# Sixteen experts' weights split by VectorE alone, and a last norm in groups of two and three tiles

## The chip, the core and the metric

The kernel runs on one core of one Trainium2 chip. The metric is the device time of one execution in microseconds (us), lower is better. Three runs of the kernel before took 2844.61, 2835.43 and 2843.97 us, a median of 2843.97.

## The reference

The reference is two transformer blocks over 1024 tokens of width 1024. The change touches only the end of the second one: a mixture of 16 experts in which every expert chooses its 128 tokens, and the norm behind it.

```python
def expert_choice_ffn(h, router_w, w_gate, w_up, w_down):
    cap = EC_CAPACITY * t // N_EXPERTS                    # 2 * 1024 / 16 = 128
    aff = softmax(h @ router_w)
    vals, idx = top_k(swapaxes(aff, 1, 2), cap)           # per expert: its 128 tokens
    xs = h[idx]
    hid = silu(xs @ w_gate) * (xs @ w_up)                 # three 1024 x 1024 matrices
    out = (hid @ w_down) * vals                           # per expert
    return zeros((t, d)).at[idx].add(out)
...
    x = x + g2 * expert_choice_ffn(hx, ...)
    return rmsnorm(x, final_g)
```

All of it is in float32.

## The kernel before, in words

A product in float32 is made of three: TensorE multiplies in a shorter float format (fp32r), so each operand is split into a high half (a copy rounded to that format) and a low half (what is left), and high x high, high x low and low x high are added up in PSUM.

The weights of an expert come in twelve pieces of 1 MB, `[128, 2048]` in float32: four of the gate matrix, four of the up matrix, four of the down matrix. `piece` (lines 254 to 261) loads one through the queue of SyncE into a tile `raw`; ScalarE makes the high half `whi` (line 266); the low half `wlo` is a subtraction (line 269), on VectorE or on GpSimd by the argument `le`. In `product` (line 1784) the pieces 0, 1 and 2 of each matrix have their low half from VectorE and piece 3 has it from GpSimd. Then twelve matmuls of 512 columns use the piece (lines 1792 to 1794). There are eight raw buffers, four for high halves and four for low halves (`k.streams(wp, 8, 4, 4, 2048)`, line 1749). A raw buffer is free for the next load when both halves are made, a half's buffer when TensorE has used it.

Per expert, `route` makes a one-hot matrix on VectorE (`oh`), sixteen narrow matmuls turn it into row numbers and values (`pid`), and GpSimd issues a gather of the 128 rows of `hx` (tile `xg`, 0.5 MB). `to_cm` transposes eight blocks on TensorE and splits them (`xth`, `xtl`). `gate_up` runs the gate product into `pg`, a tanh on ScalarE into `th` (line 1801), a multiply on VectorE (line 1802), the up product into `pu`, and the product of both, `hid`. `to_cm` turns `hid` as well (`hth`, `htl`), and `down` runs the down product of the expert before into `pd`, scales it into `o` on VectorE and lets GpSimd issue a scatter that adds 0.5 MB to the residual in memory. Routing runs three experts ahead.

`last_norm` (line 1837) loads eight tiles of 128 tokens and calls `tm_norm` for each: a sum of squares on ScalarE, a reciprocal root by three Newton steps in `rsqrt` (line 282) on VectorE, a scaling with the gain on VectorE, a store.

The order of the instructions on each engine is fixed when the kernel is built, by a scheduler that simulates the program; what comes later on an engine waits for what stands ahead of it. Which row follows which is thus not in the code, and a small edit can change the order of the whole stage.

Of the kernel before, what the change touches and what calls it, by code (L numbers as in the profile page):

```python
# [7 lines left out]
F32 = mybir.dt.float32  # L8
# [5 lines left out]
OP = mybir.AluOpType  # L14
# [952 lines left out]
def tm_norm(k, pool, xs, gain, shift):  # L967

    nc = k.nc
    n = len(xs)  # L970
    ms = pool.tile([128, n], F32, tag="tms", name="tms")
    junk = pool.tile([128, 1024], F32, tag="njunk", name="tjunk")
# [648 lines left out]
def moe(k, lc):  # L1621
# [126 lines left out]
    wp = lc.enter_context(k.pool("wm"))  # L1748
    k.streams(wp, 8, 4, 4, 2048)
    mb = lc.enter_context(k.pool("mb", side="right"))  # L1750
# [3 lines left out]
    def route(e):  # L1754
# [9 lines left out]
        ts(val, ps[:, 1:2], 0.5, None, op0=OP.mult)  # L1764
        x = mb.tile([128, 1024], F32, tag="xg", bufs=3, name="xg")
        nc.gpsimd.indirect_dma_start(out=x, out_offset=None, in_=d_hx,
# [16 lines left out]

    def product(ps, src, e, h, l, pool=(3,)):
        for p in range(4):
            wh, wl = k.piece(src[e, p], le="pool" if p in pool else "dve")
            for q in range(2):
# [8 lines left out]
    def gate_up(e, h, l):  # L1796
        pg, pu = k.acc("pg"), k.acc("pu")
        hv = lambda z: (z[:, 0:512], z[:, 512:1024])
        product(hv(pg), A["w_g"], e, h, l)
        th = mb.tile([128, 1024], F32, tag="th", name="th")  # L1800
        act(th, pg, AF.Tanh, scale=0.5)
        stt(th, th, 1.0, pg, op0=OP.add, op1=OP.mult)
        product(hv(pu), A["w_u"], e, h, l)
        hid = mb.tile([128, 1024], F32, tag="hid", name="hid")
        for sl in H2:
            tt(hid[:, sl], th[:, sl], pu[:, sl], op=OP.mult)
        return hid

# [10 lines left out]

    R = [route(e) for e in range(3)]  # L1820
    xt = to_cm(R[0][2], "xt")
    prev = None
    for e in range(NE):
# [6 lines left out]
        prev = (e, *to_cm(hid, "ht"), ids, val)  # L1830
        if e + 3 < NE:
            R.append(route(e + 3))
    down(*prev)
# [3 lines left out]
def last_norm(k, d_x3, out):  # L1837
    nc, tc, A = k.nc, k.tc, k.A
    with k.pool("ln") as ln:
        fg = row_bcast(k, ln, A["fg2"], "fg")  # L1840
        for t in range(8):
            z = ln.tile([128, 1024], F32, tag="z", bufs=8, name="z")
            (nc.sync if t % 2 else nc.scalar).dma_start(z, d_x3[128 * t:128 * t + 128, :])
            tm_norm(k, ln, [z], fg, None)
            (nc.scalar if t % 2 else nc.sync).dma_start(out[128 * t:128 * t + 128, :], z)

# [38 lines left out]
```

## Time and profile before

| what | us |
|---|---|
| median of three runs | 2843.97 |
| the profiled execution, its own time | 2840.99 |
| its span in the trace | 2839.1 |
| TensorE busy in the span | 2412.9 (85%) |
| VectorE busy | 1749.7 (62%) |
| ScalarE busy | 1193.3 (42%) |
| GpSimd busy | 1107.7 (39%) |
| low halves on VectorE, 144, busy | 451.1 |

The profile is of one execution, 3 us below the median of the runs. Its shares are means over stages of different kinds, so they say little on the experts; the windows and timelines of the rows below are of that stage and of the last norm alone. In them PE is TensorE, PEld its weight loads, DVE VectorE, ACT ScalarE, POOL GpSimd and SP SyncE. Times are counted from the start of the span. PEclk is the granted clock of TensorE as a share of 2.4 GHz; it has two levels, 1.2 and 2.4 GHz, and a value between is a mean over the window.

### The profile page before, as it was taken

What the parts mean: (1) busy time and instruction counts of PE and PEld (TensorE: products, weight loads), DVE (VectorE), ACT (ScalarE), POOL (GpSimd) and SP (SyncE); (2) the same over time, 40 slices, a digit from 0 to 9 for tenths busy, and PEclk for the clock granted to TensorE, in tenths of its full rate; (3) what the DMA queues carried; (4) which work ended last, traced back from release to release, by engine and by line L of the source; (5) the groups of instructions that cost most, each with busy time, mean ns of one, the idle gap of its engine ahead of it and who ended that gap; (6) DMA issues with size and microseconds to landing.
All of it is one profiled execution on the core that took longest, in us unless ns stands there. A gap on an engine that the chain in (4) does not pass through costs nothing. (4 is left out here: it accounts for less than half of the span.)

```text
span 2839.1 us, 40542 instructions
## 1 busy us (share of the span) xinstructions
PE 2412.9 (85%) x15678; PEld 1982.2 (70%) x15678; DVE 1749.7 (62%) x2631; ACT 1193.3 (42%) x1973; POOL 1107.7 (39%) x863
## 2 busy tenths in 40 slices
PE   5789997888689976989997778889958999999982
PEld 4556786677568965877776666667847887777772
DVE  7064727766323375122657768564776998899885
ACT  3133432222222152324636665632324666556562
POOL 5111214432344255342636454342313545444442
PEclk8879997888889987999985665669968999999996
DMA  4355321111254332435212122257455999998884
GB/s 179 53 185 171 105 82 46 36 62 53 86 179 137 134 117 95 157 134 156 77 58 77 40 75 66 65 168 235 171 237 195 369 368 340 319 324 320 328 324 141
DMA packets 220284, 458.53 MB, mean 162 GB/s; under 512 B 45631, under 2 KB 139903, under 8 KB 195516
## 3 DMA queue, kind: packets, MB, share of 16 engines
q1 hardware_dynamic: 203868, 406.80, 41.7%
q0 software_dynamic: 6240, 21.10, 2.8%
q10 hardware_dynamic: 9984, 28.05, 2.5%
q8 instruction: 123, 2.02, 0.3%
q14 instruction: 69, 0.57, 0.1%
HBM read 370.03 MB, written 77.22 MB: 158 GB/s over the span
## 5 line engine op out<-in xcount | busy, mean ns | idle before, releaser
L269 POOL TENSOR_TENSOR wlo<-raw,whi 128x1024 fp32r<-128x1024 f32 (+1 forms) x135 | 451.7, 3348 | 762.0 <-ACT whi L266 741.1
L266 ACT ACTIVATE whi<-raw 128x2048 fp32r<-128x2048 f32 (+1 forms) x279 | 456.0, 1648 | 446.0 <-PE prest L278 94.8
L269 DVE TENSOR_TENSOR wlo<-raw,whi 128x2048 fp32r<-128x2048 f32 x144 | 451.1, 3163 | 54.2 <-ACT whi L266 54.2
L277 PE MATMUL prest<-hTh,whi 128*128 128x512 f32 x448 | 181.8, 406 | 4.4 <-ACT ev L376 4.4
L278 PE MATMUL prest<-hTl,whi 128*128 128x512 f32 x448 | 178.4, 398 | 0.0
L279 PE MATMUL prest<-hTh,wlo 128*128 128x512 f32 x448 | 178.1, 398 | 0.0
L1793 PE MATMUL pg<-wlo,xth 128*128 128x512 f32 x256 | 109.7, 428 | 28.9 <-POOL wlo L269 25.7
L1794 PE MATMUL pg<-whi,xtl 128*128 128x512 f32 x256 | 107.6, 420 | 2.5 <-DVE xtl L1781 2.5
L1792 PE MATMUL pg<-whi,xth 128*128 128x512 f32 x256 | 108.4, 423 | 0.0
L863 DVE SCALAR_TENSOR_TENSOR ac<-raw,sc,ac 128x1024 f32<-128x1024 f32 x64 | 91.4, 1442 | 26.2 <-DMA raw<-in_ada_w 23.5
L1793 PE MATMUL pd<-wlo,hth 128*128 128x512 f32 x256 | 102.1, 399 | 5.0 <-DVE wlo L269 4.6
L277 PEld LDWEIGHTS prest<-hTh,whi 128*128 128x128 f32 x448 | 86.9, 194 | 23.7 <-ACT ev L376 5.3
L1793 PE MATMUL pu<-wlo,xth 128*128 128x512 f32 x256 | 101.1, 395 | 0.0
L1794 PE MATMUL pu<-whi,xtl 128*128 128x512 f32 x256 | 100.6, 393 | 0.0
L1794 PE MATMUL pd<-whi,htl 128*128 128x512 f32 x256 | 100.5, 393 | 0.0
L1792 PE MATMUL pu<-whi,xth 128*128 128x512 f32 x256 | 100.4, 392 | 0.0
L279 PEld LDWEIGHTS prest<-hTh,wlo 128*128 128x128 f32 x448 | 86.4, 193 | 18.8
L278 PEld LDWEIGHTS prest<-hTl,whi 128*128 128x128 f32 x448 | 86.4, 193 | 17.4
L1792 PE MATMUL pd<-whi,hth 128*128 128x512 f32 x256 | 92.5, 394 | 2.5 <-ACT whi L266 2.5
L469 DVE CUSTOM_DVE_ANT_0 sc<-psc,bt 128x384 f32<-128x384 f32 (+1 forms) x64 | 32.7, 520 | 99.4 <-DMA bt<-d_f 52.4
L277 PE MATMUL px<-h2h,whi 128*128 128x512 f32 x224 | 90.6, 404 | 1.2 <-ACT px L1022 1.2
L1031 DVE SCALAR_TENSOR_TENSOR mix<-px,omu,mix 128x1024 f32<-128x1024 f32 (+1 forms) x23 | 23.2, 1013 | 110.8 <-ACT mix L1030 107.4
(583 smaller groups left out, 6883.9 us busy)
## 6 DMA issues: line engine op xcount, KB each, us to landing
raw<-in_w_g SPq DMA_DIRECT2D x64, 1024.0 KB, 6.0
raw<-in_w_u SPq DMA_DIRECT2D x64, 1024.0 KB, 6.9
raw<-in_w_d SPq DMA_DIRECT2D x64, 1024.0 KB, 6.2
raw<-in_w_in SPq DMA_DIRECT2D x69, 512.0 KB, 3.4
raw<-in_ada_w SPq DMA_DIRECT2D x48, 512.0 KB, 3.3
x<-in_x SPq DMA_DIRECT2D x16, 512.0 KB, 5.8
d_g<-ev SPq DMA_DIRECT2D x32, 256.0 KB, 3.1
gt<-d_g SPq DMA_DIRECT2D x16, 512.0 KB, 5.0
```

The lines of the kernel that those rows point to most:

```text
L266: nc.scalar.activation(hi, src, AF.Copy)
L269: (nc.gpsimd if le == "pool" else nc.vector).tensor_tensor(lo, src, hi.bitcast(F32), op=OP.subtract)
L277: mm(ps, wh[:, c], xh[:, kt, sl], start=kt == 0, stop=False)
L278: mm(ps, wh[:, c], xl[:, kt, sl], start=False, stop=False)
L279: mm(ps, wl[:, c], xh[:, kt, sl], start=False, stop=kt == kts - 1)
L469: nc.vector.tensor_tensor_reduce(sc[:, :W], pss[g][:, :W], bt[:, 4 * g + i, c0:c1], 1.0, -3e38, op0=OP.add, op1=OP.max, accum_out=MX[g][:, ...
L863: nc.vector.scalar_tensor_tensor(ac, raw, sc[:, 8 * w + p:8 * w + p + 1], ac, op0=OP.mult, op1=OP.add)
L1031: nc.vector.scalar_tensor_tensor(xv, body[:, :, 0:W], k.omu[:, mu:mu + 1], xv, op0=OP.mult, op1=OP.add)
L1792: mm(o, h[:, kt], wh[:, c], start=kt == 0, stop=False)
L1793: mm(o, h[:, kt], wl[:, c], start=False, stop=False)
L1794: mm(o, l[:, kt], wh[:, c], start=False, stop=kt == 7)
```

## The change

Five edits, four of them in the expert stage:

- All low halves of the experts' weights are made by VectorE; `product` loses its argument.
- The ring of raw tiles has eleven buffers instead of eight; the rings of high and of low halves have three instead of four.
- Two gathered tiles `xg` instead of three, and routing runs two experts ahead instead of three.
- `hid` has no tile of its own: the product of `th` and `pu` is written over `th`.
- `last_norm` loads its eight tiles first, and calls `tm_norm` for groups of 2, 3 and 3 tiles; `tm_norm` then makes the reciprocal roots of a group in one chain on tiles of two and three columns. The tile of mean squares gets two buffers per group size.

```diff
@@ tm_norm
-    ms = pool.tile([128, n], F32, tag="tms", name="tms")
+    ms = pool.tile([128, n], F32, tag=f"tms{n}", bufs=2, name="tms")
@@ moe
-    k.streams(wp, 8, 4, 4, 2048)
+    k.streams(wp, 11, 3, 3, 2048)
...
-        x = mb.tile([128, 1024], F32, tag="xg", bufs=3, name="xg")
+        x = mb.tile([128, 1024], F32, tag="xg", bufs=2, name="xg")
...
-    def product(ps, src, e, h, l, pool=(3,)):
+    def product(ps, src, e, h, l):
         for p in range(4):
-            wh, wl = k.piece(src[e, p], le="pool" if p in pool else "dve")
+            wh, wl = k.piece(src[e, p], le="dve")
...
         product(hv(pu), A["w_u"], e, h, l)
-        hid = mb.tile([128, 1024], F32, tag="hid", name="hid")
         for sl in H2:
-            tt(hid[:, sl], th[:, sl], pu[:, sl], op=OP.mult)
-        return hid
+            tt(th[:, sl], th[:, sl], pu[:, sl], op=OP.mult)
+        return th
...
-    R = [route(e) for e in range(3)]
+    R = [route(e) for e in range(2)]
...
-        if e + 3 < NE:
-            R.append(route(e + 3))
+        if e + 2 < NE:
+            R.append(route(e + 2))
@@ last_norm
+        xs = []
         for t in range(8):
             z = ln.tile([128, 1024], F32, tag="z", bufs=8, name="z")
             (nc.sync if t % 2 else nc.scalar).dma_start(z, d_x3[128 * t:128 * t + 128, :])
-            tm_norm(k, ln, [z], fg, None)
-            (nc.scalar if t % 2 else nc.sync).dma_start(out[128 * t:128 * t + 128, :], z)
+            xs.append(z)
+
+        t = 0
+        for n in (2, 3, 3):
+            tm_norm(k, ln, xs[t:t + n], fg, None)
+            for i in range(t, t + n):
+                (nc.scalar if i % 2 else nc.sync).dma_start(out[128 * i:128 * i + 128, :], xs[i])
+            t += n
```

The order of the instructions up to the expert stage is the same in both kernels. In it, the scheduler orders every engine anew. On VectorE, in the middle of the stage, from the multiply behind one expert's tanh, before:

```order
L1802 SCALAR_TENSOR_TENSOR th<-th,pg 128x1024
L269 TENSOR_TENSOR wlo<-raw,whi 128x2048
L1806 TENSOR_TENSOR hid<-th,pu 128x512 x2
L269 TENSOR_TENSOR wlo<-raw,whi 128x2048 x2
L1781 TENSOR_TENSOR htl<-ptc,hth 128x512 x2
L269 TENSOR_TENSOR wlo<-raw,whi 128x2048
L1763 CAST ids<-pid 128x1
L1764 TENSOR_SCALAR val<-pid 128x1
L1756 TENSOR_TENSOR oh<-rcst,slotT 128x1024
L269 TENSOR_TENSOR wlo<-raw,whi 128x2048
```

and in the changed kernel, from the same multiply of an expert in the middle (the second `th` is the product written over it, `o` is made of the two PSUM tiles `pd`):

```order
L1802 SCALAR_TENSOR_TENSOR th<-th,pg 128x1024
L269 TENSOR_TENSOR wlo<-raw,whi 128x2048 x4
L1805 TENSOR_TENSOR th<-th,pu 128x512 x2
L269 TENSOR_TENSOR wlo<-raw,whi 128x2048 x3
L1814 SCALAR_TENSOR_TENSOR o<-pd_20423,val,g_17672 128x512
L269 TENSOR_TENSOR wlo<-raw,whi 128x2048
L1814 SCALAR_TENSOR_TENSOR o<-pd_20424,val,g_17672 128x512
L269 TENSOR_TENSOR wlo<-raw,whi 128x2048
L1781 TENSOR_TENSOR xtl<-ptc,xth 128x512 x2
L1781 TENSOR_TENSOR htl<-ptc,hth 128x512
L269 TENSOR_TENSOR wlo<-raw,whi 128x2048
L1781 TENSOR_TENSOR htl<-ptc,hth 128x512
```

Twelve low halves an expert stand there instead of nine, four of them instead of one between the multiply and the product with `pu`; and pairs like `xtl` and `htl` come next to each other.

On TensorE, where the stage begins, one set of row-number matmuls less stands ahead of the first transposes:

```order
 L1743 MATMUL psl<-cst,nm 128x128
-L1760 MATMUL pid<-ta,oh 128x2 x24
+L1760 MATMUL pid<-ta,oh 128x2 x16
 L1778 MATMUL ptc<-cst,xg 128x128 x8
 L1792 MATMUL pg<-whi,xth 128x512
```

The third set and each later one comes in the gate product of the expert before the one it is for. In two of the early experts 61 matmuls of 512 columns stand between it and the transposes of the rows gathered by it; in the others more, in the kernel before a whole expert more.

On VectorE, where the last norm begins, behind the last scaling of a down product, before:

```order
L1815 SCALAR_TENSOR_TENSOR o<-pd_23006,val,g_17672 128x512
L975 TENSOR_SCALAR tms<-tms 128x1
L288 TENSOR_SCALAR rsi<-tms 128x1
L289 TENSOR_SCALAR rsy<-rsi 128x1
L292 TENSOR_SCALAR rst<-rsy,tms 128x1
L296 TENSOR_SCALAR rst<-rst 128x1
L297 TENSOR_TENSOR rsy<-rsy,rst 128x1
```

and in the changed kernel, where one chain serves two tiles:

```order
L1814 SCALAR_TENSOR_TENSOR o<-pd_22987,val,g_17672 128x512
L975 TENSOR_SCALAR tms<-tms 128x2
L288 TENSOR_SCALAR rsi<-tms 128x2
L289 TENSOR_SCALAR rsy<-rsi 128x2
L294 TENSOR_TENSOR rst<-rsy 128x2
L295 TENSOR_TENSOR rst<-rst,tms 128x2
L296 TENSOR_SCALAR rst<-rst 128x2
L297 TENSOR_TENSOR rsy<-rsy,rst 128x2
```

A chain has twelve small instructions before and fifteen after; there were eight chains and there are three.

## Rows read from the trace of the kernel before

**Rows 1.** The timeline of ScalarE: start us, us, engine, line, operation, out<-in, count, [idle before <-releaser]
```profile
2187.46 1.03 ACT L1801 ACTIVATE th<-pg 128x1024 f32<-128x1024 f32 x1 [0.80 <-PE pg L1794]
...
2375.24 1.03 ACT L1801 ACTIVATE th<-pg 128x1024 f32<-128x1024 f32 x1 [0.33 <-PE pg L1794]
...
2755.49 1.02 ACT L1801 ACTIVATE th<-pg 128x1024 f32<-128x1024 f32 x1 [6.01 <-PE pg L1794]
```

**Rows 2.** Windows of one expert: window, us; per engine busy us (instructions); PEclk, DMA share, GB/s
```profile
2263.20:2300.40 37.20, 36.74 (x179) 30.36 (x178) 34.30 (x22) 25.82 (x18) 19.20 (x6) 1.00 0.98 370
2506.40:2549.20 42.80, 39.37 (x177) 31.95 (x177) 38.92 (x22) 25.53 (x17) 18.98 (x5) 0.93 0.92 324
```

**Rows 3.** The timeline of all engines where the expert stage begins
```profile
2136.87 10.37 PE L1760 MATMUL pid<-ta,oh 128*128 128x2 f32 x48 [1.72 <-DVE oh L1756]
...
2152.62 0.39 PE L1792 MATMUL pg<-whi,xth 128*128 128x512 f32 x1
...
2152.82 1.92 ACT L266 ACTIVATE whi<-raw 128x2048 fp32r<-128x2048 f32 x1 [3.13 <-PE pg L1794]
...
2154.77 2.29 DVE L269 TENSOR_TENSOR wlo<-raw,whi 128x2048 fp32r<-128x2048 f32 x1 [4.36 <-ACT whi L266]
...
2160.55 0.39 PE L1794 MATMUL pg<-whi,xtl 128*128 128x512 f32 x1
```

**Rows 4.** The timeline of TensorE, early expert: transposes, row-number matmuls
```profile
2283.79 1.03 PE L1778 MATMUL ptc<-cst,hid 128*128 128x128 f32 x8
...
2292.86 1.84 PE L1760 MATMUL pid<-ta,oh 128*128 128x2 f32 x16
```

**Rows 5.** The timeline of all engines in a late expert
```profile
2538.55 7.69 DVE L269 TENSOR_TENSOR wlo<-raw,whi 128x2048 fp32r<-128x2048 f32 x1
...
2538.95 5.13 POOL L269 TENSOR_TENSOR wlo<-raw,whi 128x2048 fp32r<-128x2048 f32 x1
...
2544.13 0.79 PE L1793 MATMUL pg<-wlo,xth 128*128 128x512 f32 x1 [2.82 <-POOL wlo L269]
```

**Rows 6.** The tile raw, VectorE: duration ns min/median/max, first and last start us
```profile
L269 DVE TENSOR_TENSOR wlo<-raw,whi x144: 2273/2281/7710, 2086.2 to 2780.9; 128x2048 fp32r<-128x2048 f32 x144
```

**Rows 7.** Groups by line and form, VectorE: count | busy us, mean ns | idle before
```profile
L269 DVE TENSOR_TENSOR wlo<-raw,whi 128x2048 fp32r<-128x2048 f32 x144 | 451.1, 3163 | 54.2 <-ACT whi L266 54.2
...
L295 DVE TENSOR_TENSOR rst<-rst,tms 128x4 f32<-128x4 f32 x6 | 1.0, 162 | 0.2
```

**Rows 8.** The waits of ScalarE, 2080 to 2800 us: us in total, times, longest
```profile
ACT whi L266 <- DMA raw<-in_w_g: 3.8, 2, 2.1
```

**Rows 9.** The timeline of VectorE in an early expert
```profile
2314.39 1.28 DVE L1781 TENSOR_TENSOR xtl<-ptc,xth 128x512 fp32r<-128x512 f32 x2
...
2327.00 1.40 DVE L1815 SCALAR_TENSOR_TENSOR o<-pd,val,g 128x512 f32<-128x512 f32 x2
...
2335.40 0.15 DVE L1763 CAST ids<-pid 128x1 uint32<-128x1 f32 x1
...
2336.67 2.28 DVE L269 TENSOR_TENSOR wlo<-raw,whi 128x2048 fp32r<-128x2048 f32 x1
2338.87 1.21 DVE L1802 SCALAR_TENSOR_TENSOR th<-th,pg 128x1024 f32<-128x1024 f32 x1
```

**Rows 10.** DMA issues, 2320 to 2360 us: count, median us to landing
```profile
xg<-d_hx,ids POOLq DMA_INDIRECT x1, 12.7
```

**Rows 11.** The timeline of ScalarE, then of VectorE, in the last norm
```profile
2803.54 1.06 ACT L974 ACTIVATE tjunk<-z 128x1024 f32<-128x1024 f32 x1 [23.20 <-DMA z<-d_x]
...
2807.42 1.28 DVE L978 SCALAR_TENSOR_TENSOR z<-z,rsy,fg 128x1024 f32<-128x1024 f32 x1
2808.62 0.15 DVE L975 TENSOR_SCALAR tms<-tms 128x1 f32<-128x1 f32 x1
...
2834.26 1.28 DVE L978 SCALAR_TENSOR_TENSOR z<-z,rsy,fg 128x1024 f32<-128x1024 f32 x1
```

**Rows 12.** Windows, as in the second group: the first pieces are loaded
```profile
2090.00:2094.00 4.00, 2.48 (x11) 2.21 (x12) 3.85 (x5) 1.34 (x3) 0.00 (x0) 0.50 1.02 430
```

## The prediction

> **What bounds the kernel now.** I read the 40 slices of the page first: from the 31st on TensorE and VectorE are 8 to 9 tenths busy and the DMA moves over 300 GB/s. That is the expert stage, and all that the change touches lies there and in the last norm behind it.
>
> Then the stage by itself. Each expert has one tanh on ScalarE after its gate product; from the second (2187.46) to the sixteenth (2755.49) are 568.0 us, 14 intervals, a mean of 40.57 us [rows 1]. They are of two kinds. The first five, up to 2375.24, take 37.6 on average, the last nine 42.3. The windows of one expert each show the difference [rows 2]: from 2263.2 on 37.2 us, TensorE busy for 36.7 and its granted clock 1.00 (2.4 GHz); from 2506.4 on 42.8, TensorE idle for 3.4 and its clock 0.93.
>
> What is TensorE's floor? An expert has 144 matmuls of 512 columns. Between 2152.62 and 2160.55 stand 35 of them at full clock: 0.2266 us each [rows 3], so 32.6 us. Two sets of eight transposes at 1.03 and sixteen row-number matmuls at 1.84 [rows 4] make 36.5 us. The early pattern is 0.6 us above that floor, the late window 6.3.
>
> Why the later one? In the waits TensorE stands longest before a low half of a weight that GpSimd writes: 2.82 us at 2544.13 [rows 5]. With one such stall an expert the 6.3 us are explained: 2.8 of stall, and a mean clock of 0.93 says that 0.07 / 0.5 = 14% of the window, 6.0 us, ran at the lower level of 1.2 GHz, which loses 3.0 more. The cause is seen in the same rows: a low half on VectorE, begun at 2538.55, takes 7.69 us while GpSimd's own runs 5.13 us beside it; without such company the median is 2.281 us [rows 6]. The 144 low halves of VectorE take 451.1 us [rows 7]; at 2.281 they would take 328.5. So 122.6 us of VectorE's time is nothing but waiting for GpSimd's reads.
>
> Weights in transit do not bound it: ScalarE waited 3.8 us in all for a raw piece [rows 8].
>
> **The change part by part.**
>
> *Low halves.* 48 of 192 go from GpSimd to VectorE (three of twelve an expert). VectorE's new work per expert: from the start of a lone low half to the next instruction is 2.20 us (2336.67 to 2338.87), twelve are 26.4; row numbers, values and one-hot 1.27 (2335.40 to 2336.67); three pairs like xtl, at 1.28 less the 0.08 by which neighbours overlap, 3.6; the pair o 1.32; the multiply after the tanh 1.13 [rows 9]. Sum 33.7 us, below TensorE's 36.5. Before, it was 38.9 us in a late expert [rows 2]. So VectorE takes on 48 instructions and still gets lighter, since GpSimd no longer reads anything in this stage; TensorE stays the bound.
>
> The Trainium skill speaks against this: its page Perfetto Trace Analysis, section Optimizing Scalar/DVE Operations, says that a saturated VectorE may do well to hand work to ScalarE or even GpSimd. That page of the Trainium skill adds that the two share a read port, so that it might not help. Rows 5 and 6 side with the addition; had the first half held, the time would be that of the fifth rival below.
>
> *Rings of three instead of four for high and low halves.* This is the price. A high half may be written when TensorE is through with the piece whose buffer it takes. Rows 3 show that loop uncontended: TensorE ends the first piece at 2152.8, ScalarE starts at 2152.82 (1.92 us), VectorE at 2154.77 (2.29 us), ready at 2157.06; TensorE wants it four pieces after the first began, right behind the last matmul at 2160.55, so about 2161.0. Margin 3.9 us. With three buffers it is one piece (2.72 us) less: 1.2 us. VectorE's other jobs push into this: a pair of 1.2 to 1.4 us between two low halves, less the 0.5 us that VectorE has free per piece, costs 0.9 of the 1.2. Two pairs in a row, which the new order has once or twice an expert, cost 1.4 to 2.1: a stall of 0.2 to 0.9 us. The tanh delays the next high half by 1.03 us, but the multiply on VectorE then runs beside that high half. So I expect up to 0.6 us of stalls an expert; the first window of rows 2 has 0.46 us of idle TensorE in it and kept a clock of 1.00. Bounds: 0 to 5 us an expert. I take the pace of the early pattern, 37.1 us, which has the floor plus 0.6: 14 x (40.57 - 37.1) = 48.6 us saved.
>
> *Raw ring of eleven.* ScalarE hardly waited for raw pieces, so three more hide little: 0 to 3.8 us [rows 8]; I take 0. The DMA must move 12.6 MB of weights and 1.05 MB of gather and scatter in 37.1 us, 368 GB/s, which the early pattern did [rows 2].
>
> *Two gathered tiles instead of three.* Routing one expert less ahead removes eight of the 24 pairs of row-number matmuls before the first product, at most a third of 10.37 us [rows 3]. The first gather has to land too, so I take 1.5 us of the 0 to 3.4. The other side: a gather is now used within the same expert. In two early experts 61 matmuls, 13.8 us, stand between its row numbers and its transposes, and it lands 12.7 us after its issue [rows 10], with up to 1 us before that. Bounds 0 to 6 us of stall; I take 2.
>
> *hid into th.* The product overwrites th, so the next tanh waits for the transposes of it; in the new order those stand half a product or more ahead of it on TensorE. Nothing; if they came late, ScalarE would be held behind them and the loop above with it.
>
> *Last norm.* VectorE's chain alone sets this end. Eight tiles are 3.83 us apart (2807.42 to 2834.26 in seven steps): 1.20 us of scaling, to 2808.62, and 2.64 us for twelve small instructions, 0.22 each [rows 11]. After: three rounds of 15 at 0.22 (a form of four columns takes 0.162 us [rows 7], no more than one column), 9.9, and eight scalings, 9.6: 19.5 instead of 30.7, 11.2 less. The first round waits for a second sum of squares, 1.06 us on ScalarE [rows 11] and its read-out. I take 10.0 us. The last three stores are now 1.2 us apart instead of 3.8, which may give back some tenths.
>
> Sum: 48.6 - 2 + 1.5 + 10.0 = 58.1 us. The profiled execution took 2840.99 us, span 2839.1; 2841.0 - 58.1 = 2782.9. The median of the runs shown is 2843.97, 3 us above it and within their spread of 9 us.
>
> **The rivals.**
>
> 1. *The rings of three stall.* If every expert has two or three stalls of 1 us, as two-pair places with a late high half would give, the pace is 38.5 to 41.5 us: 2802 to 2844 us, say 2817 at 39.6. For it: a margin of 1.2 us against pairs of 1.3. Against it: in the new order each wait of VectorE on TensorE is for the same piece whose end also frees the next high half, so the two run side by side.
> 2. *The clock goes with it; slower than before.* Place: two pairs in a row on VectorE before a low half. Price: when such a stall grows to the 2.82 us of 2544.13 [rows 5], the lower clock after it costs 3.0 more, as worked out from rows 2. At 1.3 such places an expert the pace is 36.5 + 1.3 x 5.8 = 44.0 and the time 2841 + 14 x 3.4 - 9.5 = 2879. It decides from a pace of 41.3 on, where the stage gives back what start and end gain. Against it: GpSimd's 5 us splits made that stall, and they are gone.
> 3. *Transfers become the bound.* At the floor, 13.65 MB in 36.5 us are 374 GB/s. With the DMA share at 0.98 in the early window [rows 2] it may be at its end at 370, a pace of 36.9: nothing lost. The Trainium skill's page SBUF — State Buffer, section Summary: rules for kernel authors, puts HBM to SBUF transfers at about 358 GB/s; by it, an estimate, the pace would be 38.1 and the time 2797; the trace does not agree. Against it: 430 GB/s while the first pieces were loaded [rows 12].
> 4. *Only the end moves.* If the later pattern's stalls have another cause than GpSimd, the stage stays and 2830 remains. The 2.82 us row names GpSimd, so this is unlikely.
> 5. *VectorE keeps its mean of 3.16 us a low half* [rows 7]. Then an expert has 12 x 3.13 + 7.3 = 45 us of VectorE and the time is about 2890. Against it: a median of 2.281 in the same row as the 7.71.
>
> **How the numbers follow.** Forecast, pace 36.5 to 38.5, 2766 to 2802: 0.62. Rival 1: 0.20, a tenth of it within 0.3% of before. Rival 2: 0.06. Rival 3: 0.05. Rival 4: 0.05. Rival 5: 0.02. About 0.3%, 8.5 us, is what a measurement of this kernel can tell. Faster: 0.62 + 0.18 + 0.05 + 0.05 = 0.90; same 0.02; slower 0.08. Low end: the floor of 36.5 in all 14 intervals (57 us), 3.4 at the start, 11.2 at the end give 2769, less 3 for the spread of the runs. High end: 2818, the middle of rival 1. Between lies nearly 0.8.
>
> **What would show it.** Right: tanh to tanh near 37 us up to the last expert; a clock of 0.98 or more in those windows; 192 low halves on VectorE with a mean under 2.35 us; GpSimd with gathers and scatters alone; 11 to 12 us less from the first to the last scaling in the last norm. Wrong: waits of TensorE for low halves summing to over 30 us, with high halves behind them waiting on TensorE; transposes waiting for a gather in more than two experts; ScalarE waiting for raw pieces.

## The result, and the profile after

The changed kernel takes 2799.84 us (median of four runs, 2797.09 to 2807.33). Four runs of the kernel before, beside it, have a median of 2841.09. The ratio is 0.9864, with a 95% interval of 0.9844 to 0.9884: faster by 1.4%, some 41 us. The forecast was 2782.9 with a range of 2766 to 2818. So the sign and the range hold, but 17 us of the expected 58 did not come.

The two profiled executions, 2840.99 and 2797.09 us, are compared stretch by stretch. The marks are the matmul psl, which ends the routing tables, the tanhs of [rows 1], the last output product's o, and the span's end:

| stretch | before, us | after, us | difference, us | forecast, us |
|---|---|---|---|---|
| start to psl (same program) | 2134.7 | 2139.0 | +4.3 | 0 |
| psl to the second tanh | 52.8 | 49.7 | -3.1 | -1.5 |
| second to sixteenth tanh, 14 intervals | 568.0 | 535.5 | -32.5 | -46.6 |
| sixteenth tanh to the last o | 35.7 | 34.2 | -1.5 | 0 |
| last o to the end | 47.9 | 36.9 | -11.0 | -10.0 |

The shortfall lies in the 14 intervals: 14.1 us. Here are the tanhs that end them on both sides, in the timeline of ScalarE of the changed kernel, to be held against [rows 1]:

```profile
2188.68 1.03 ACT L1801 ACTIVATE th<-pg 128x1024 f32<-128x1024 f32 x1 [1.03 <-PE pg L1794]
...
2724.17 1.03 ACT L1801 ACTIVATE th<-pg 128x1024 f32<-128x1024 f32 x1 [1.02 <-PE pg L1794]
```

The intervals, in order: 38.14, 36.37, 36.38, 36.42, 37.30, **42.54**, 36.37, **42.46**, 36.35, **42.32**, 36.55, 37.30, **42.29**, 34.70. They are not spread around the forecast of 37.1. Eight are 36.35 to 37.30, better than the forecast or within 0.2 us of it, and four cost 42.3 to 42.5. The windows of one expert of each kind, after (columns as in [rows 2]):

```profile
2299.60:2336.00 36.40, 36.40 (x177) 30.38 (x176) 34.75 (x25) 25.75 (x18) 5.16 (x2) 1.00 1.00 384
2373.29:2415.83 42.54, 38.34 (x177) 31.61 (x176) 33.80 (x25) 26.01 (x17) 5.16 (x2) 0.96 0.94 343
```

In the first TensorE is busy for all of 36.40 us. In the second it idles for 4.2, and its granted clock is 0.96. What it waited for, between 2130 and 2770 us (us in total, times, longest):

```profile
PE ptc L1778 <- DVE xtl L1781: 12.1, 6, 2.6
PE pg L1792 <- ACT xth L1780: 6.4, 4, 1.6
...
PE pd L1793 <- DVE wlo L269: 0.3, 1, 0.3
```

TensorE's waits for low halves are gone (0.3 us), and VectorE's low halves have lost their company; the tile's group on VectorE after, against [rows 6, 7] (duration in ns: least, median, most):

```profile
L269 DVE TENSOR_TENSOR wlo<-raw,whi x192: 2278/2287/2296, 2090.6 to 2754.1; 128x2048 fp32r<-128x2048 f32 x192
```

In their place stands a new wait, at the transposes of gathered rows and the split (xth, xtl) of what they give. This is TensorE's timeline in the expert of 42.54 us:

```profile
2394.63 0.40 PE L1794 MATMUL pd<-whi,htl 128*128 128x512 f32 x1
2394.86 1.04 PE L1778 MATMUL ptc<-cst,xg 128*128 128x128 f32 x8
2397.51 0.50 PE L1792 MATMUL pg<-whi,xth 128*128 128x512 f32 x1 [1.61 <-ACT xth L1780]
2397.85 0.40 PE L1793 MATMUL pg<-wlo,xth 128*128 128x512 f32 x1
2400.84 0.92 PE L1778 MATMUL ptc<-cst,th 128*128 128x128 f32 x4 [2.59 <-DVE xtl L1781]
...
2402.41 0.63 PE L1793 MATMUL pg<-wlo,xth 128*128 128x512 f32 x1
```

The eight transposes of xg stand behind the last matmul of the output product and directly in front of the gate product that needs them. TensorE has nothing else in its order, so it sits through the whole chain: 1.61 us for xth, then 2.59 for xtl. ScalarE comes to xth late, because in its order a high half of a weight stands ahead of it; this high half itself began when TensorE was through with an earlier piece:

```profile
2395.06 1.91 ACT L266 ACTIVATE whi<-raw 128x2048 fp32r<-128x2048 f32 x1 [0.81 <-PE pd L1794]
2396.88 1.07 ACT L1780 ACTIVATE xth<-ptc 128x512 fp32r<-128x512 f32 x2
```

VectorE comes to xtl late as well, because in its order two low halves and an o come first:

```profile
2395.04 2.28 DVE L269 TENSOR_TENSOR wlo<-raw,whi 128x2048 fp32r<-128x2048 f32 x1
2397.24 0.74 DVE L1814 SCALAR_TENSOR_TENSOR o<-pd,val,g 128x512 f32<-128x512 f32 x1
2397.90 2.28 DVE L269 TENSOR_TENSOR wlo<-raw,whi 128x2048 fp32r<-128x2048 f32 x1
2400.10 1.28 DVE L1781 TENSOR_TENSOR xtl<-ptc,xth 128x512 fp32r<-128x512 f32 x2
```

Windows around that place (columns as before) show what the clock added:

```profile
2398.20:2400.80 2.60, 0.04 (x1) 0.00 (x0) 2.60 (x3) 0.00 (x0) 2.54 (x1) 1.00 1.03 366
2400.80:2404.50 3.70, 3.66 (x11) 3.04 (x12) 1.27 (x2) 0.60 (x1) 0.84 (x1) 0.54 0.99 343
2404.50:2407.20 2.70, 2.70 (x13) 2.21 (x12) 0.00 (x0) 1.78 (x1) 0.00 (x0) 1.00 1.01 296
```

After 2.6 us in which TensorE was busy for 0.04, it is granted 0.54 for 3.70 us, near the lower level of 1.2 GHz: 3.70 x 0.46 = 1.7 us lost. With the 4.2 of waiting that is 5.9 us, the difference between 42.4 and 36.4. The windows of all four such experts have a clock of 0.96: together 24 us.

They are not waiting for the gather: this tile's gather was issued at 2370.85 and landed 9.5 us later, about 14 us before its transposes ran. Behind the first expert the least time between a landing and its transposes was 1.3 us.

Start and end did a little more than forecast. At the start TensorE has 32 row-number matmuls instead of 48, but the transposes behind them then wait 2.25 us (put down to oh, which was done 0.8 us earlier; the gather, issued at 2145.84, landed 4.3 us later, just before they began):

```profile
2141.17 6.96 PE L1760 MATMUL pid<-ta,oh 128*128 128x2 f32 x32 [1.72 <-DVE oh L1756]
2150.37 1.94 PE L1778 MATMUL ptc<-cst,xg 128*128 128x128 f32 x8 [2.25 <-DVE oh L1756]
```

So the first product gained nothing: its tanh came 26.3 us behind psl before and 26.8 after. The gain lies between the first tanh and the second, 26.44 us before and 22.87 after. The first tanh, before and after:

```profile
2161.03 1.03 ACT L1801 ACTIVATE th<-pg 128x1024 f32<-128x1024 f32 x1 [0.85 <-PE pg L1794]
2165.81 1.03 ACT L1801 ACTIVATE th<-pg 128x1024 f32<-128x1024 f32 x1 [0.80 <-ACT xth L1780]
```

At the end, VectorE's last o and the three groups of scalings, against [rows 11]:

```profile
2758.37 1.43 DVE L1814 SCALAR_TENSOR_TENSOR o<-pd,val,g 128x512 f32<-128x512 f32 x2 [1.98 <-PE pd L1794]
...
2776.04 2.48 DVE L978 SCALAR_TENSOR_TENSOR z<-z,rsy,fg 128x1024 f32<-128x1024 f32 x2
...
2781.88 3.68 DVE L978 SCALAR_TENSOR_TENSOR z<-z,rsy,fg 128x1024 f32<-128x1024 f32 x3
...
2787.84 3.68 DVE L978 SCALAR_TENSOR_TENSOR z<-z,rsy,fg 128x1024 f32<-128x1024 f32 x3
```

### The profile page after: what moved, and what is told of

Its sections match the earlier page's. It is cut to its first block, busy times and chain, and to the rows that moved or that the text cites. A ratio compares the mean times of both kernels' runs of the same rounds, so it can differ in the third digit from the quotient of the medians.

```text
span 2795.3 us, 40451 instructions
## 1 busy us (share of the span) xinstructions
PE 2400.2 (86%) x15678; PEld 1979.2 (71%) x15678; DVE 1712.1 (61%) x2628; ACT 1197.3 (43%) x1973; POOL 873.1 (31%) x815
## 4 chain that ended last, share of the span: by engine, by line
PE 55%; DVE 19%; ACT 6%; DMA 5%; issue 5%; POOL 3%; SPq 0%; ACTq 0%; DVEq 0%; POOLq 0%
PE pg L1794 2%; PE pg L1792 2%; PE pg L1793 2%; PE px L277 2%; PE px L278 2%; PE px L279 2%; PE pu L1793 2%; PE pu L1792 2%; PE pu L1794 2%; PE prest L277 2%; PE prest L278 2%; PE prest L279 1%; DVE wlo L269 1%; PE pd L1794 1%; PE pd L1793 1%
## 5 line engine op out<-in xcount | busy, mean ns | idle before, releaser
L269 DVE TENSOR_TENSOR wlo<-raw,whi 128x2048 fp32r<-128x2048 f32 x192 | 435.8, 2288 | 59.3 <-ACT whi L266 58.8
L269 POOL TENSOR_TENSOR wlo<-raw,whi 128x1024 fp32r<-128x1024 f32 x87 | 216.6, 2492 | 491.7 <-ACT whi L266 468.5
L1815 POOL DMA_INDIRECT d_x<-o,ids x16 | 51.6, 3227 | 417.7 <-DVE o L1814 417.7
L1793 PE MATMUL pg<-wlo,xth 128*128 128x512 f32 x256 | 102.8, 402 | 0.0
L469 DVE CUSTOM_DVE_ANT_0 sc<-psc,bt 128x384 f32<-128x384 f32 (+1 forms) x64 | 32.6, 519 | 95.4 <-DMA bt<-d_f 52.6
```

Source lines behind the costliest of these rows:

```text
L269: (nc.gpsimd if le == "pool" else nc.vector).tensor_tensor(lo, src, hi.bitcast(F32), op=OP.subtract)
L469: nc.vector.tensor_tensor_reduce(sc[:, :W], pss[g][:, :W], bt[:, 4 * g + i, c0:c1], 1.0, -3e38, op0=OP.add, op1=OP.max, accum_out=MX[g][:, ...
L1793: mm(o, h[:, kt], wl[:, c], start=False, stop=False)
L1815: nc.gpsimd.indirect_dma_start(out=d_x3, out_offset=bass.IndirectOffsetOnAxis(ap=ids[:, :1], axis=0), in_=o, in_offset=None, compute_op=OP ...
```

## The experiments

The theory: GpSimd's low halves were the cost that the change removes, and the four late experts come from where the transposes of gathered rows stand. With route(e+2) called at the end of expert e's turn, the scheduler, so the theory goes, takes the gather to be late and puts the transposes behind the output product; what the scheduler reckons with is on no record. Rivals: the rings of three halves, the raw ring, the weights' transfers, the count of gathered tiles.

Eleven kernels ran. The stretch up to psl, the same program in all but the last two rows, began its last matmul anywhere from 2127.9 to 2146.7 us, so the stretches behind it tell more than the whole time. The time is the median of all runs of a kernel, and the ratio is to runs of the kernel before beside them (medians 2840.18 to 2846.53); psl and the stretches are of the one profiled execution. All in us:

| kernel | time, median | ratio to before, 95% | psl | psl to 2nd tanh | 14 intervals | 16th tanh to end |
|---|---|---|---|---|---|---|
| before | | | 2134.7 | 52.8 | 568.0 | 83.6 |
| after | 2799.84 | 0.9864 (0.9844 to 0.9884) | 2139.0 | 49.7 | 535.5 | 71.1 |
| e1_dve | 2792.93 | 0.9826 (0.9807 to 0.9845) | 2142.0 | 51.2 | 515.2 | 83.2 |
| e3_norm | 2836.98 | 0.9986 (0.9969 to 1.0003) | 2139.7 | 54.7 | 563.9 | 73.4 |
| e4_xg3 | 2769.80 | 0.9754 (0.9729 to 0.9778) | 2127.9 | 50.2 | 513.9 | 70.9 |
| e6_xg3_844 | 2784.07 | 0.9788 (0.9768 to 0.9808) | 2131.4 | 52.6 | 515.0 | 72.5 |
| e7_raw8 | 2792.35 | 0.9805 (0.9774 to 0.9836) | 2139.0 | 50.5 | 529.5 | 72.2 |
| e5_ring844 | 2797.77 | 0.9828 (0.9798 to 0.9857) | 2144.4 | 51.8 | 531.2 | 72.4 |
| e10_early | 2781.35 | 0.9780 (0.9753 to 0.9806) | 2146.7 | 55.0 | 513.1 | 70.8 |
| e2_pool3 | 2865.52 | 1.0074 (1.0049 to 1.0099) | 2138.9 | 53.0 | 590.8 | 81.6 |
| e11_r833 | 2854.12 | 1.0031 (1.0014 to 1.0048) | 2136.8 | 53.9 | 571.1 | 90.9 |
| e8_rw | 2885.15 | 1.0127 (1.0092 to 1.0162) | 2174.7 | 69.4 | 576.5 | 71.0 |
| e9_wo | 2790.00 | 0.9800 (0.9768 to 0.9832) | 2152.8 | 50.1 | 516.0 | 70.9 |

**e1_dve: the low halves alone.**

```diff
-            wh, wl = k.piece(src[e, p], le="pool" if p in pool else "dve")
+            wh, wl = k.piece(src[e, p], le="dve")
```

> The kernel before with one edit: VectorE makes every low half; the ring of eight raw tiles, the rings of four halves, the three gathered tiles and the old last norm stay. Theory (the low half is worth the pace, and what the change lost, about 6 us in each of four experts, comes from gathering only two experts ahead): the low halves take 2.29 us each, no wait of TensorE on them is left, and all 14 intervals between tanhs come out at 36.3 to 37.3 us, none at 42; the stage loses 14 x 4.1 = 57 us and about 3 at its start, so the time is 2841 - 60 = 2781 us (2774 to 2790). Rival A (the raw ring of eight is too short for a VectorE that no longer waits, so TensorE waits for weights): intervals of 38 to 40, 2800 to 2825 us. Rival B (the four late experts come from the memory, not from the gathers): intervals of 42 appear here too, in 3 to 5 experts, and the time is 2800 to 2812 us.

One edit takes 52.8 us from the 14 intervals, more than the whole change did (32.5). No interval is longer than 38.3, though three are above the 37.3 that I expected. One expert's window:

```profile
2267.94:2304.37 36.43, 36.43 (x177) 30.34 (x176) 34.17 (x25) 25.77 (x17) 5.16 (x2) 1.00 1.00 378
```

Both rivals fall. The time itself is 12 us above what was expected and outside its range; 7 of these lie before psl in the profiled execution, where nothing was changed.

**e3_norm: the last norm alone** (the buffers of the means in tm_norm, and last_norm, on the kernel before).

```diff
-            tm_norm(k, ln, [z], fg, None)
...
+        for n in (2, 3, 3):
+            tm_norm(k, ln, xs[t:t + n], fg, None)
```

> The kernel before with the last norm of the change alone (tiles in groups of two, three and three, two buffers for the means). Theory: the time from the last output product's o to the span's end falls from 47.9 to 37 us, and nothing before it moves: 2841 - 11 = 2830 us (2826 to 2834), a ratio of 0.996. Rival (the end is set by the last scatters and the reload of d_x3, so the norm itself is hidden): 0.999 to 1.000, and the stretch after the last o stays above 45 us.

The last o stands at 2794.00, and the span ends at 2831.7: 37.7 us, 10.2 less than before. The scalings, in VectorE's timeline, follow as in the changed kernel:

```profile
2794.00 1.43 DVE L1815 SCALAR_TENSOR_TENSOR o<-pd,val,g 128x512 f32<-128x512 f32 x2 [8.05 <-PE pd L1794]
2812.22 2.48 DVE L978 SCALAR_TENSOR_TENSOR z<-z,rsy,fg 128x1024 f32<-128x1024 f32 x2
...
2824.27 3.68 DVE L978 SCALAR_TENSOR_TENSOR z<-z,rsy,fg 128x1024 f32<-128x1024 f32 x3 [0.29 <-DVE rsy L297]
```

In the trace the term is as expected. The whole time is inconclusive: its median lies 3 us above its range, and its interval takes in 1.000 and just misses the expected 0.996. e1_dve and e6_xg3_844, which run the stage alike (515.2 and 515.0 us) and differ in this norm, are 8.9 us apart.

**e4_xg3 and e6_xg3_844: three gathered tiles again**, with rings of (10, 3, 3), and of (8, 4, 4).

```diff
-        x = mb.tile([128, 1024], F32, tag="xg", bufs=2, name="xg")
+        x = mb.tile([128, 1024], F32, tag="xg", bufs=3, name="xg")
...
-    R = [route(e) for e in range(2)]
+    R = [route(e) for e in range(3)]
...
-        if e + 2 < NE:
-            R.append(route(e + 2))
+        if e + 3 < NE:
+            R.append(route(e + 3))
```

> The changed kernel with three gathered tiles and routes three experts ahead as before the change, a raw ring of ten (11 doesn't fit beside the third tile) and rings of three halves. Theory (an expert takes 42 us where the transposes of the gathered rows stand directly in front of the gate product that uses them, and they stand there because the gather is placed only two experts ahead): the transposes stand inside the output product in all experts, no interval of 42 us is left, all are 36.3 to 37.3, and the time is 2797 - 4 x 6 = 2773 us (2768 to 2781). Rival A (the rings of three halves make the late experts): three to five intervals of 42 stay, 2793 to 2803 us. Rival B (the weights' transfers make them): the same times as rival A, with TensorE's waits ended by a DMA.

> The changed kernel with three gathered tiles, routes three ahead and the rings of before (eight raw, four and four halves): so the change without its rings and without its two gathered tiles. Theory (the gathers decide, the rings do nothing): the same as the run with ten raw tiles, within 4 us: 2773 us (2768 to 2781), intervals of 36.3 to 37.3. Rival A (the rings of three halves make the late experts): this one is faster than the run with rings of three by 15 us or more. Rival B (the longer raw ring is worth something once VectorE makes all low halves): this one is slower than the run with ten raw tiles by 8 us or more, with waits of TensorE ended by DMA.

Both stages came out alike, 513.9 and 515.0 us in the 14 intervals, with none over 39.2: the rings of three cost nothing here, and the longer raw ring gives nothing. (They differ in both rings at once, so one could hide what the other does.) The transposes no longer wait for xtl; the largest wait of TensorE left in e4_xg3 is small:

```profile
PE pg L1793 <- DVE wlo L269: 4.9, 5, 1.4
```

e4_xg3 came out within its range. e6_xg3_844 is 3 us above its own and its median 14 us above that of e4_xg3, which rival B would have at 8 or more; but no wait of TensorE in the stage is ended by a DMA, as rival B wants, and the two ratios' intervals overlap. Of the 8.6 us between the two profiled executions 3.5 lie before psl, 4.0 in the start and the end and 1.1 in the 14 intervals; the rest of the 14 is not explained. e4_xg3, at 0.9754, beats both kernels, and its interval does not touch that of the changed kernel.

**e7_raw8: two gathered tiles, transposes elsewhere.** The raw ring goes from eleven to eight, and with it the scheduler's order: the transposes now stand 10 to 36 matmuls before the end of the output product.

```diff
-    k.streams(wp, 11, 3, 3, 2048)
+    k.streams(wp, 8, 3, 3, 2048)
```

> The changed kernel with a raw ring of eight in place of eleven, and nothing else: two gathered tiles and rings of three halves as in the change. In its order on TensorE the transposes of gathered rows stand inside the output product in all experts but the first, with at least 10 matmuls of that product behind them, and never directly in front of the gate product. Theory (the place of these transposes makes the four late experts, not the count of gathered tiles by itself): no interval of 42 us is left, the 14 intervals sum to 512 to 520 us (changed kernel 535.5; three gathered tiles 513.9), and the time is 2797 - 18 = 2779 us (2768 to 2788). Rival A (the gather itself is late with two tiles, wherever the transposes stand): TensorE waits for the gathered tile or behind it, and the sum stays at 530 us or more. Rival B (eleven raw tiles are needed once VectorE makes all low halves): intervals of 38 to 40 with waits ended by DMA, a sum of 535 or more.

No interval of 42 is left, but the sum is 529.5: my 512 to 520 was too low, and so was the range of the time. Four intervals are 39.48, each where 12 matmuls of the product follow the transposes. TensorE, then VectorE, in one of them:

```profile
2470.38 1.03 PE L1778 MATMUL ptc<-cst,xg 128*128 128x128 f32 x8
...
2476.51 0.50 PE L1793 MATMUL pg<-wlo,xth 128*128 128x512 f32 x1 [1.68 <-DVE wlo L269]
```
```profile
2471.64 0.69 DVE L1781 TENSOR_TENSOR xtl<-ptc,xth 128x512 fp32r<-128x512 f32 x1 [2.04 <-ACT xth L1780]
...
2474.17 2.28 DVE L269 TENSOR_TENSOR wlo<-raw,whi 128x2048 fp32r<-128x2048 f32 x1
```

VectorE comes to xtl in its order and idles 2.04 us for the late transposes, with a low half queued behind; TensorE then waits 1.68 us for that low half. So late transposes hurt along a second path. The distance on TensorE alone does not decide: one expert with 10 matmuls behind them took 36.23 us. The rivals as put do not hold either, though the sum is close to that of rival A: in the intervals one wait of TensorE, of 0.7 us, is ended by the gather, and none by a weight's transfer.

**e5_ring844: two gathered tiles, long rings of halves** (the changed kernel with the rings of before).

```diff
-    k.streams(wp, 11, 3, 3, 2048)
+    k.streams(wp, 8, 4, 4, 2048)
```

> The changed kernel with the rings of before (eight raw, four and four halves); two gathered tiles as in the change. In its order on TensorE the transposes of gathered rows stand directly in front of the gate product in five experts, with one matmul between in a sixth and four in a seventh (changed kernel: four). Theory (that place costs about 6 us each time): five to seven intervals of 41 to 43 us, a sum of 14 intervals of 509 + 5.5 x 6 = 542 us (538 to 552), and a time of 2797 + 7 = 2804 us (2798 to 2818), although its rings of halves are longer. Rival A (the rings of three halves make the late experts): the sum falls to 512 to 518 us, as in the runs with three gathered tiles.

531.2 us, between theory and rival. Three intervals of 40.3 to 40.4 and two of 38.6 to 38.8 show the late place; none is 42. One of them, in the timelines of TensorE, ScalarE and VectorE, and its expert's window:

```profile
2520.77 0.50 PE L1792 MATMUL pg<-whi,xth 128*128 128x512 f32 x1 [0.25 <-ACT xth L1780]
...
2523.29 0.76 PE L1778 MATMUL ptc<-cst,th 128*128 128x128 f32 x4 [1.78 <-DVE xtl L1781]
```
```profile
2520.12 1.09 ACT L1780 ACTIVATE xth<-ptc 128x512 fp32r<-128x512 f32 x2 [1.24 <-PE ptc L1778]
```
```profile
2520.35 2.28 DVE L269 TENSOR_TENSOR wlo<-raw,whi 128x2048 fp32r<-128x2048 f32 x1
2522.55 1.28 DVE L1781 TENSOR_TENSOR xtl<-ptc,xth 128x512 fp32r<-128x512 f32 x2
```
```profile
2497.92:2538.32 40.40, 38.37 (x177) 31.59 (x176) 34.44 (x25) 26.01 (x17) 5.16 (x2) 0.96 0.97 342
```

The waits are 0.25 and 1.78 us, where the changed kernel has 1.61 and 2.59. The same place on TensorE costs 6 us in the changed kernel and 2 to 4 here. So short rings do not make the late experts. Their price goes by what stands ahead of the splits: here ScalarE waits for the transposes and takes xth at once, and VectorE has one low half behind their start ahead of xtl; in the changed kernel a high half stands ahead of xth, and two low halves and an o ahead of xtl. Rings and orders changed together, and no run tells which of the two sets the price.

**e10_early: two gathered tiles, the route called earlier.**

```diff
     for e in range(NE):
+        if e + 2 < NE:
+            R.append(route(e + 2))
         ids, val, x = R[e]
...
-        if e + 2 < NE:
-            R.append(route(e + 2))
```

> The changed kernel (eleven raw tiles, rings of three, two gathered tiles) with one edit: route(e+2) is called at the head of expert e's turn, before its gate product, not at the end of the turn. The tile that it fills was last read by the transposes for expert e, so it is free by then. On TensorE the transposes of gathered rows then stand inside a product everywhere, with at least ten matmuls behind them. Theory (the place of the gather and of the transposes makes the late experts, neither the count of gathered tiles nor the rings of halves): no interval of 42 us is left, 14 intervals sum to 513 to 518 us (changed kernel 535.5, three gathered tiles 513.9), and the time is 2797 - 20 = 2777 us (2766 to 2784). Rival A (two gathered tiles are too few, wherever the route stands): TensorE's transposes wait for the gathered tile, or intervals of 39 to 42 stay, and the sum is 525 us or more. Rival B (with rings of three and late transposes, as in the run with eight raw tiles, VectorE falls behind): intervals of 39.5 with waits of TensorE for low halves, a sum of 525 to 532 us.

513.1 us, the lowest of all, with the changed kernel's rings and two tiles. An expert's window:

```profile
2313.46:2349.84 36.38, 36.38 (x177) 30.39 (x176) 34.38 (x25) 25.78 (x18) 5.94 (x2) 1.00 0.98 368
```

So neither the rings nor the count of tiles by itself makes the late experts; where the route is called does. The call moves two things, the gather's time and the order; since the gathers had landed in time in the changed kernel too, the order is what is left. The start gives some back (55.0 us to the second tanh, as expert 2's row numbers now stand ahead of the end of the first gate product). The median of 2781.35 us is above that of e4_xg3, but the two ratios' intervals overlap.

**e2_pool3 and e11_r833: GpSimd's low halves with the short rings.** The first gives the last piece of each product back to GpSimd in the changed kernel; the second gives the kernel before rings of (8, 3, 3).

```diff
-            wh, wl = k.piece(src[e, p], le="dve")
+            wh, wl = k.piece(src[e, p], le="pool" if p == 3 else "dve")
```

> The changed kernel with GpSimd making the low half of each product's last piece again (48 of 192), rings, gathered tiles and last norm as in the change. Theory (GpSimd's low half blocks VectorE while it runs and itself comes late): VectorE's low halves beside it take up to 7.7 us again, TensorE waits for low halves 2 to 4 us in an expert, 14 intervals sum to 555 to 575 us (changed kernel 535.5, before 568.0), so the time is 2797 + 30 = 2827 us (2815 to 2840). Rival (the longer raw ring does the change's work, and who makes the low half matters little): 2795 to 2805 us.

> The kernel before with one edit: rings of three halves in place of four (eight raw tiles, three gathered tiles, GpSimd's low half of every last piece, the old norm all stay). Theory (a ring of three is too short when GpSimd makes a low half and VectorE is kept out beside it, though it costs nothing when VectorE makes them all): the 14 intervals sum to 580 to 592 us (before 568.0), as in the run of the changed kernel with GpSimd's low half (590.8), and the time is 2841 + 18 = 2859 us (2850 to 2868). Rival A (what made that run slow is the two gathered tiles): the sum stays at 566 to 572 us and the time at 2836 to 2846 us.

e2_pool3 is slower than the kernel before, beyond my range: without the low halves on VectorE the rest of the stage's edits are a loss of 22.8 us in the 14 intervals. e11_r833 shows that rings of three alone are not that loss: 571.1 against 568.0, so rival A was nearer, though the time came out where the theory had it (7 us of it behind the last tanh). But they change the pattern: 40.7 us already in the early experts, which took 37.1 before, by waits for GpSimd's low halves:

```profile
PE pg L1793 <- POOL wlo L269: 25.5, 14, 2.8
PE pu L1793 <- POOL wlo L269: 12.8, 13, 1.0
```

e2_pool3, with two gathered tiles, is 19.7 us longer in the intervals than e11_r833 with three, much like the changed kernel against its runs with three (some 21). Both causes stand side by side in it, the second being the transposes again:

```profile
PE pg L1793 <- POOL wlo L269: 13.5, 8, 2.3
PE ptc L1778 <- DVE xtl L1781: 13.0, 6, 2.6
```

**e8_rw and e9_wo: idle work on GpSimd.** On e4_xg3 with a raw ring of nine, 48 GpSimd instructions on a tile dm that nothing else reads: a subtraction, or a fill.

```diff
             wh, wl = k.piece(src[e, p], le="dve")
+            if p == 3:
+                nc.gpsimd.tensor_tensor(dm, dm, dm, op=OP.subtract)    # e8_rw
+                nc.gpsimd.memset(dm, 0.0)                              # e9_wo
```

> The changed kernel with three gathered tiles, routes three ahead and a raw ring of nine, and one addition: beside the last piece of each product (48 times) GpSimd subtracts a 128x2048 tile from itself, in place, a tile that nothing else reads. VectorE still makes every low half, so no product waits for GpSimd. Theory (VectorE is kept out while GpSimd works on such a tile): VectorE's low halves beside it stretch from 2.29 to as much as 7.4 us, three times an expert, VectorE's 32 us an expert become 40 to 47, and it sets the pace: 40 to 46 us, 2820 to 2910 us. Rival (in the kernel before, the low halves of GpSimd were only late in coming, and VectorE's long ones waited for something else): low halves of 2.29 us, a pace of 36.4 to 37 and 2765 to 2785 us.

> The run with GpSimd's idle subtraction again (three gathered tiles, nine raw tiles, VectorE makes all low halves), but GpSimd now only fills the idle tile with zeros, 48 times: it writes 128x2048 and reads nothing. Theory (VectorE is kept out by GpSimd's reading of two tiles, in turns of one low half for each subtraction): with the reads gone low halves stay at 2.29 us, the 14 intervals sum to 512 to 520 us and the time is 2768 to 2785 us. Rival (any GpSimd work on such a tile keeps VectorE out, for as long as it runs): low halves of 3 to 6 us beside the fills, and the intervals in the stretch of the fills are 39 to 55 us as with the subtraction.

Nothing holds these instructions, so GpSimd ran them early: the subtractions fill the first five experts, which take 41 to 56 us; from then on the pace is 36.4 to 37.8. VectorE, then GpSimd, then the window, among the subtractions:

```profile
2305.26 20.78 DVE L269 TENSOR_TENSOR wlo<-raw,whi 128x2048 fp32r<-128x2048 f32 x4
```
```profile
2292.22 37.28 POOL L1790 TENSOR_TENSOR dm<-dm 128x2048 f32<-128x2048 f32 x7
```
```profile
2305.26:2325.96 20.70, 13.58 (x44) 9.44 (x42) 20.70 (x5) 7.65 (x4) 20.39 (x5) 0.83 0.53 197
```

Four low halves take 20.78 us, 5.2 each; a GpSimd subtraction takes 5.3, and 3.60 where VectorE has no such work beside it. They go one for one, though no data connects them. How they do so shows ahead of the stage, where VectorE has small instructions. GpSimd, then VectorE:

```profile
2113.89 3.60 POOL L1790 TENSOR_TENSOR dm<-dm 128x2048 f32<-128x2048 f32 x1
```
```profile
2114.61 0.15 DVE L296 TENSOR_SCALAR rst<-rst 128x1 f32<-128x1 f32 x1
2114.80 2.70 DVE L297 TENSOR_TENSOR rsy<-rsy,rst 128x1 f32<-128x1 f32 x1
```

A subtraction runs from 2113.89 to 2117.49. Beside it VectorE's instruction on one tile of one column takes 0.15 us, but the product of two such tiles takes 2.70 (one of four columns 0.162, [rows 7]) and ends at 2117.50, with the subtraction. So here VectorE's instruction with two tiles is not slowed but waits until GpSimd's has ended. The time, 2885.15 us, lies in the theory's range partly by this: of 129 us between the profiled executions of e8_rw and e4_xg3, 47 lie before psl and 63 in the intervals.

Among the fills, GpSimd, then VectorE:

```profile
2169.00 20.56 POOL L1790 MEMSET dm<- 128x2048 f32 x11
```
```profile
2182.90 6.77 DVE L269 TENSOR_TENSOR wlo<-raw,whi 128x2048 fp32r<-128x2048 f32 x3
```

The fills, 1.8 us each, leave VectorE's low halves at 2.28 to 2.29. This is shown for the nine low halves that ran beside fills; 31 of the 48 fills began before psl, where GpSimd's copies for the routing tables stood behind fills (TensorE waited 4.8 us for one, and psl came at 2152.8). The median, 2790.00 us, is above what was expected.

## Why the prediction was right in sign and short in size

- **Low halves to VectorE: right.** The reading of [rows 5 to 7], that VectorE lost 122.6 us to GpSimd's company and not to work of its own, held: 192 low halves have a mean of 2.288 us, and e1_dve gains more in the stage by this edit than the change. e8_rw shows the mechanism by itself, and e9_wo that a fill, which reads nothing, does not have it.
- **The pace of 37.1 us: the floor and some tenths of stall, a little too high.** The mean was 38.25, but not by a higher floor: where no expert is late the 14 intervals take 513.1 us (e10_early), 36.65 each, where 14 x 37.1 would be 519. By this term the change would have saved 55 us and not 48.6.
- **Two gathered tiles, "I take 2" of "0 to 6 us of stall": the step that failed.** It cost 21.6 to 22.4 us (535.5 less the 513.9 of e4_xg3 and the 513.1 of e10_early). That is 20 more than taken, and less the 6 of the pace it is the 14 us that are missing. The forecast asked whether the gathered tile would have landed, and at two early experts only. Behind the first expert it had landed each time. What was late were the transposes, which the new order puts directly in front of the gate product in four later experts, with the splits on ScalarE and VectorE behind other work. The forecast counted the 61 matmuls between a gather and its use in two early experts, but the order changes along the stage.
- **Rings of three: right, and rival 1 wrong**, though the time came close to its lower end. With all low halves on VectorE and no late transposes they cost nothing (513.9 against 515.0 us). Whether the margin of 1.2 us that the forecast worried about adds to a late place, 6 us here and 2 to 4 in e5_ring844, the runs do not tell.
- **hid into th, the raw ring of eleven: nothing that shows**, as taken. e1_dve keeps hid apart and runs the stage as e6_xg3_844 does. ScalarE's waits for raw pieces, before it makes high halves, did not get less: 5.4 us in the window of [rows 8], 1.6 of them from 2130 on, against 3.8 before.
- **Rival 2, the clock:** its mechanism is there, at another place and too small to turn the sign: 1.7 us in each of four experts.
- **Rival 3, the transfers.** It named 2797 us by the Trainium skill's page SBUF — State Buffer, section Summary: rules for kernel authors, and the result is 2799.84. That is chance: by its 358 GB/s every expert would need 38.1 us, an estimate, yet eight took 36.35 to 37.30, one of them at 384 GB/s. The measurement decides against that page of the Trainium skill here.
- **Rival 4 and rival 5** fell with e1_dve.
- **Last norm: right**, -11.0 for -10.0. **Start: right in number, not in its mechanism.** The -3.1 for -1.5 did not come from fewer row-number matmuls, which the wait for the first gather ate up. It came between the first tanh and the second: 26.44 us before, 25.1 in the three runs with VectorE's low halves and rings of four, and 22.9 in the five with VectorE's low halves and rings of three (e8_rw, with its subtractions there, left aside).
- **The time** lies in the forecast's own band, 2766 to 2802, and the mean pace in its 36.5 to 38.5. That is partly luck: the band stood for small stalls in every expert, and what came was none in most and 6 us in four. A fifth late expert would have left it. Of the signs that the forecast named, the mean of the low halves (under 2.35) came; the pace near 37 up to the last expert and the clock of 0.98 or more failed in those four (42.4 and 0.96).

## What to carry to other kernels

When an edit changes how far ahead something is fetched, ask not only whether the data have landed, but where the consumer's instructions then stand in the order of every engine, expert by expert: a short chain of three engines directly in front of the product that needs it cost here two fifths of what the main edit won in the stage (22 of 53 us). Split a change of several parts: one line of it gave the stage more than all of them together, and the place of a call took two fifths of that back. And an engine that helps another may cost it more time than it saves: look at the longest instance of the helped engine's instruction, not at the median.

## What was not expected of the hardware

- VectorE's subtraction and GpSimd's, both of 128x2048, run one for one at 5.2 to 5.3 us although they share no data; alone VectorE's takes 2.28 and GpSimd's 3.60. Even a product of two tiles of one column, 128x1, took 2.70 us on VectorE beside GpSimd's subtraction. GpSimd's fill of the same size does not hold VectorE's low halves up.
- The weights came in at 384 GB/s over one expert of 36.40 us, with a DMA share of 1.00, so the transfers may be close to being the next bound. That is not shown: at a share of 1.02 the first pieces came at 430 GB/s [rows 12].
- The same program up to psl took from 2127.9 to 2146.7 us in different executions. The runs do not tell why; a difference of under 10 us between two kernels is better read from the stretch that was changed.
